# Expert stage of a transformer layer: TensorE in program order with whole blocks, last w2 loads ahead of the norm's, gain rows spread by a matmul

## The chip, the cores and the metric

The kernel runs on one core of one Trainium2 chip. A core has a matrix engine (TensorE, PE in the profile, with its weight loads shown as PEld), three engines for elementwise work (VectorE = DVE, ScalarE = ACT, GpSimd = POOL) and SyncE (SP), which here issues nearly all DMA transfers. The metric is device time in microseconds (us) of one execution of the whole layer.

## The reference

One trunk layer, fp32, 512 latent rows of 1024 channels and 256 context rows. First a token mixer (latent attention and differential attention side by side, gated, one output projection), then a norm, then a mixture of 16 experts with expert choice: each expert takes the 64 rows with its largest affinity.

```python
def ec_moe(h, w_router, b_router, w1, w3, w2):
    cap = EC_CAPACITY * n // N_EXPERTS                       # 64
    aff = softmax(h @ w_router + b_router)
    g, idx = lax.top_k(jnp.swapaxes(aff, 1, 2), cap)
    xe = h[bidx, idx]                                        # 16 experts x 64 rows x 1024
    hid = silu(xe @ w1) * (xe @ w3)                          # 1024 x 1024 each
    ye = (hid @ w2) * g[..., None]
    return zeros_like(h).at[bidx, idx].add(ye)

x = layer_norm(ALPHA * x + g1 * o_lat, ln1_g, ln1_b)         # g1, g2: gains by channel, from c
x = layer_norm(ALPHA * x + g2 * ec_moe(x * (1 + sc2) + sh2, ...), ln2_g, ln2_b)
```

The weights of the experts are 16 x 3 matrices of 4 MB, 201 MB in all; each is read once.

## The kernel before, in words

The first 574 us are the mixer, the output projection, the first norm and the router. From 574 us to the end runs the expert stage, which the change rewrites.

**Pairs.** Experts are worked through in eight pairs, since 2 x 64 rows fill the 128 rows of the array. For a pair:

- `gather`: a one-hot matrix `oh` (from DVE, L1094) multiplied with the normed rows `xn` puts the pair's rows, transposed, into `xe`: 32 products of 128x128 (L1102), 64 records in the trace.
- `up_`, once for each expert: 32 products (64 records) over sixteen pages of w1 and w3, with 64 columns of weights on half the array and 512 wide (L1140, `h<-wr,xe`); then Silu on ACT (L1145) and a product on DVE (L1146) make `hid`.
- `hid_t`: four transposes of `hid` on TensorE (L1151) and a copy by ACT (L1152) into `hidT`.
- `down`: `y<-wr,hidT` (L1159), again half the array, 16 products (32 records) an expert over eight pages.
- `back` and `scatter`: the one-hots times the gates are transposed (L1120, `ohT`); `y` is scaled by gate and by the gain row `g2b` on DVE (L1166), split into two float32r parts `ye` (ACT L75, DVE L78), and multiplied by `ohT` (L1171, whole array, 128x512): for each half of the columns four token tiles of two products. DVE adds each result tile into the accumulators `acc` (L1172).

The result tiles of gather, transposes and scatter are three PSUM buffers under one name, `mx`; `h` has three buffers too and `y` two.

**Weights.** They stream as pages of 512 KB through one DMA queue (SP's), in the order in which the products use them. 36 pages form a ring (buffers under four names); nine more lie at first in the places of tiles that are needed later (`acc0`, `ye`, `hid`, ...). `piece()` returns a page and, with `prefetch`, issues the load of the page that takes the place of one already used, so loads are issued as the program is written down and each waits on SP for its place to come free. The last pair's w2 comes by column parts (`PARTS`): 16 loads of 384 KB and 4 of 512 KB, so that each part of the output is complete as early as possible.

**The end.** Behind the last up product the tiles of `ln2_g` and `ln2_b` are loaded (L1222) into the places of `xe` and `hid`; then the last down product runs part by part (L1265), each part put back through the scatter (L1248), and the second norm follows.

**What sets the order.** The kernel is written in a tile framework. A scheduler orders each engine's instructions from their dependences and its own cost estimates; the program's order is only a preference. A DMA or an engine's instruction then runs strictly in its engine's order. The scheduler interleaves products of different steps on TensorE: records of the next pair's gather between those of the running pair's up product, and scatter products between those of the next up product.

**Rows by broadcast.** The gains `g1` and `g2` exist as single rows on partitions 0, 32, 64 and 96 of two tiles `rm`. GpSimd's library call `partition_broadcast` (L968 for `g1b`, L1187 for `g2b`) spreads them over 128 partitions. `g1b` is used in the output projection: its tiles `po` are sums over products of `yh`, `yl` with the split `w_out` pages `woh`, `wol`. For the first half of the columns DVE multiplies `po` by the gain (`r<-po,g1b`, L1007); for the second POOL scales the four `w_out` pages by it first (L888), and ACT and DVE split them (L75, L78). `xn` (L1008) is then normed, and transposed for the router (L1011). A half takes 96 products `po`.

Of the kernel before, what the change touches and what calls it, by code (L numbers as in the profile page):

```python
# [10 lines left out]
F32 = mybir.dt.float32  # L11
F32R = mybir.dt.float32r
# [40 lines left out]
def _layer(tc, A, out, opened):  # L53
# [32 lines left out]
    # ---------------------------------------------------------------- constants and small vectors  # L86
# [12 lines left out]
    ghv = cp.tile([128, KD], F32, name="ghv")       # routed input = ghv * normed + bhv  # L99
# [32 lines left out]
    dqs = [rB.tile([128, NT, 256], F32, name="dq", tag="dq", bufs=2) for _ in range(2)]      # two heads each  # L132
# [92 lines left out]
    def mod_mul(q):  # L225
        """scale and shift of 256 channels, as rows"""
# [21 lines left out]
    def x_chunk(k, ci):  # L248
        """128 channels of the latent (0) or context (1) rows: transposed, modulated, split"""
# [16 lines left out]
    for q in range(4):  # L266
        # beside the products of these channels: what makes the next
# [15 lines left out]
    # rotary tables: cos, signed sin for the keys; the query ones carry the score scale  # L283
# [42 lines left out]
    one32 = mw.tile([128, 32], F32, name="one32")  # L326
    V.memset(one32, 1.0)
# [20 lines left out]
    def mod_sum(j, wa):  # L348
# [3 lines left out]
        for g in (2 * h, 2 * h + 1):  # L352
            T.matmul(pm[32 * g:32 * g + 32, :], one32, wa[:, (g % 2) * 512:(g % 2) * 512 + 512], start=True, stop=True)
# [3 lines left out]
    def chunk(col, n, cuts, evac, at, nxt):  # L357
        """projected columns; after the tiles in `at`, a part of the modulation's rows"""
# [27 lines left out]
    # latent query and key ranks: rms norm, transpose, gain  # L386
# [55 lines left out]
    def gates(g4, at=()):  # L442
        """a quarter of the gates, transposed: weights stationary"""
# [52 lines left out]
    # score tiles are emitted one by one; between them goes the product work of the tiles before  # L496
# [13 lines left out]
    def fill(parts):  # L510
        """one score tile is out: emit one of `parts` equal shares of the waiting work"""
# [12 lines left out]
    def flush(key=None):  # L524
        """emit all the waiting work, or what has `key`"""
# [7 lines left out]
    # transposed queries and keys: even heads of the differential attention, then the latent ones | odd heads  # L533
# [21 lines left out]
    def prep_t(hd, m, nm, src, c0, t0, nn):  # L555
# [8 lines left out]
        if nm == "q1":  # L564
            # the same with the halves of the contraction swapped
# [13 lines left out]
    def mod_end():  # L579
# [13 lines left out]
        # router columns with the norm's gain, less their mean: the norm's own mean then drops out  # L593
# [744 lines left out]
```

## Time and profile before

Three executions took 1096.82, 1097.37 and 1098.73 us, median 1097.37. The profiled execution shows a span of 1094.2 us from its first to its last instruction; the page gives no other time of it.

| stretch, us | what runs | PE busy, us | DVE busy | GB/s |
|---|---|---|---|---|
| 0–440 | projections, attention | 415.61 | 242.60 | 122 |
| 440–574 | merge, output projection, norm, router | 108.14 | 76.95 | 216 |
| 574–1013 | expert pairs one to seven, start of the eighth | 429.94 | 105.47 | 396 |
| 1013–1045 | the eighth pair's up products | 30.24 | 3.79 | 15 |
| 1045–1094 | its down products, second norm | 23.44 | 26.00 | 206 |

Over the span TensorE is busy 92%, DVE 42%, ACT 25%, POOL 19%. How to read the rows further down: a timeline or waits row gives start, busy time, engine, line, operation, output<-inputs and shape, then xN for N instructions taken together, and in brackets the idle time ahead of the group and what ended it. A matrix product of fp32 operands appears as two records, one of float32r operands as one.

### The profile page before, as it was taken

Reading aid. Unit: us, or ns where it says so; the run is one execution under the profiler, and the core shown is the slowest. Engines: PE = TensorE matmul, PEld = TensorE weight load, DVE = VectorE, ACT = ScalarE, POOL = GpSimd, SP = SyncE. Lnnn points to the kernel's source line nnn. Section 1 sums busy time; section 2 is a strip of 40 time slices with the busy share of each in tenths; the row PEclk is TensorE's granted clock in tenths of the full one; section 3 lists DMA queues with packets and bytes.
Section 4 is the critical chain, followed back from the end, with each engine's and each line's share of the span. In section 5 each row is a group of like instructions: output and inputs, shape, how many; then the busy total and the mean of one; then the engine's idle time right before and its main releaser. Section 6 shows DMA issues by size and latency. Waiting matters only on the chain.

```text
span 1094.2 us, 13748 instructions
## 1 busy us (share of the span) xinstructions
PE 1007.4 (92%) x5259; PEld 630.1 (58%) x5259; DVE 454.8 (42%) x832; ACT 276.0 (25%) x551; POOL 204.4 (19%) x193
## 2 busy tenths in 40 slices
PE   6999998998899999997849999999999999999972
PEld 5888977677787777675536634444434434343331
DVE  2372377643677466463584221303022131303127
ACT  1222325244677455431210101010101010100001
POOL 2340022021675222143214200000000000000004
PEclk9999999999899999999889999999999999999997
DMA  9943357741002000176678999999999999999082
GB/s 302 288 154 106 97 169 247 243 140 39 20 20 74 20 20 21 39 269 235 245 270 304 404 329 411 409 409 409 409 409 409 409 410 408 409 410 400 14 283 97
DMA packets 101209, 266.97 MB, mean 244 GB/s; under 512 B 14020, under 2 KB 37528, under 8 KB 101144
## 3 DMA queue, kind: packets, MB, share of 16 engines
q1 hardware_dynamic: 100248, 264.52, 65.8%
q0 software_dynamic: 320, 1.05, 0.3%
q8 instruction: 41, 0.67, 0.3%
q10 hardware_dynamic: 576, 0.52, 0.1%
q14 instruction: 24, 0.20, 0.1%
HBM read 261.47 MB, written 2.10 MB: 241 GB/s over the span
## 4 chain that ended last, share of the span: by engine, by line
PE 75%; DVE 9%; DMA 5%; ACT 4%; issue 3%; POOL 2%; SPq 0%; DVEq 0%; ACTq 0%; POOLq 0%
PE h L1140 22%; PE y L1159 9%; PE mx L1102 6%; PE acc L84 4%; PE acc L83 4%; PE sc L648 4%; PE acc L82 4%; PE mx L1171 3%; PE tpb L656 3%; PE av L836 2%; DMA wa<-w_ada 2%; DMA wraw<-w_in 2%; PE y L1265 1%; PE av L772 1%; PE tp L232 1%
## 5 line engine op out<-in xcount | busy, mean ns | idle before, releaser
L1140 PE MATMUL h<-wr,xe 128*64 128x512 f32 x1024 | 250.0, 601 | 0.0
L1140 PEld LDWEIGHTS h<-wr,xe 128*64 128x64 f32 x1024 | 76.0, 136 | 110.4 <-issue 94.5
L1159 PE MATMUL y<-wr,hidT 128*64 128x512 f32 x448 | 99.6, 595 | 0.7 <-ACT hidT L1152 0.7
L1146 DVE TENSOR_TENSOR hid<-hid,h 128x512 f32<-128x512 f32 x16 | 11.0, 687 | 203.6 <-PE h L1140 203.6
L1102 PEld LDWEIGHTS mx<-oh,xn 128*128 128x128 f32 x512 | 62.7, 195 | 39.9 <-issue 38.7
L637 DVE TENSOR_REDUCE nm<-sc 128x1 f32<-128x768 f32 x64 | 61.0, 954 | 38.7 <-PE sc L648 38.2
L1115 POOL TENSOR_TENSOR oh<-oh,aff 128x512 f32<-128x512 f32 x8 | 8.4, 1049 | 361.9 <-PE mx L1102 353.1
L1102 PE MATMUL mx<-oh,xn 128*128 128x128 f32 x512 | 72.6, 289 | 1.7 <-DVE oh L1094 1.7
L1159 PEld LDWEIGHTS y<-wr,hidT 128*64 128x64 f32 x448 | 34.0, 137 | 57.8 <-issue 53.2
L638 ACT ACTIVATE P<-sc,nm 128x768 f32<-128x768 f32 x64 | 57.6, 900 | 35.0 <-DVE nm L637 26.0
L1145 ACT ACTIVATE hid<-h 128x512 f32<-128x512 f32 x16 | 9.6, 597 | 195.1 <-PE h L1140 195.1
L75 ACT ACTIVATE whi<-wraw 128x1024 fp32r<-128x1024 f32 (+1 forms) x32 | 33.5, 1046 | 99.6 <-DMA wraw<-w_in 80.9
L78 DVE TENSOR_TENSOR wlo<-wraw,whi 128x1024 fp32r<-128x1024 f32 (+1 forms) x32 | 38.7, 1211 | 43.9 <-PE acc L83 28.7
L82 PE MATMUL acc<-xlh,whi 128*128 128x512 f32 x128 | 51.0, 398 | 3.6 <-ACT whi L75 2.2
L82 PE MATMUL acc<-whi,xlh 128*128 128x512 f32 (+1 forms) x128 | 49.5, 391 | 1.0 <-ACT whi L75 1.0
L83 PE MATMUL acc<-xll,whi 128*128 128x512 f32 x128 | 50.0, 391 | 0.0
L84 PE MATMUL acc<-xlh,wlo 128*128 128x512 f32 x128 | 49.4, 394 | 0.3 <-DVE wlo L78 0.3
L84 PE MATMUL acc<-whi,xll 128*128 128x512 f32 (+1 forms) x128 | 48.8, 382 | 0.5 <-POOL xll L78 0.5
L83 PE MATMUL acc<-wlo,xlh 128*128 128x512 f32 (+1 forms) x128 | 48.8, 381 | 0.2 <-DVE wlo L78 0.2
L1172 DVE TENSOR_TENSOR acc<-acc,mx 128x512 f32<-128x512 f32 x56 | 36.0, 684 | 30.0 <-PE mx L1171 30.0
L648 PE MATMUL sc<-K,Q 96*128 96x512 f32 (+1 forms) x192 | 43.9, 355 | 1.3 <-ACT P L638 1.0
L820 POOL TENSOR_SCALAR P<-P,zm 128x768 f32<-128x768 f32 x32 | 30.0, 940 | 80.0 <-DVE zm L819 75.1
(333 smaller groups left out, 1691.4 us busy)
## 6 DMA issues: line engine op xcount, KB each, us to landing
wr<-moe_w SPq DMA_DIRECT2D x372, 512.0 KB, 10.2
wa<-w_ada SPq DMA_DIRECT2D x32, 512.0 KB, 4.0
wraw<-w_in SPq DMA_DIRECT2D x28, 512.0 KB, 4.7
wa<-w_ada SPq DMA_DIRECT2D x8, 1024.0 KB, 9.7
wr<-moe_w SPq DMA_DIRECT2D x16, 384.0 KB, 8.1
outraw<-w_out SPq DMA_DIRECT2D x8, 512.0 KB, 9.6
xq<-x SPq DMA_DIRECT2D x4, 512.0 KB, 7.9
q<-q SPq DMA_DIRECT2D x16, 128.0 KB, 2.3
```

The source lines that it names most:

```text
L75: S.activation(hi, src, AF.Copy)
L78: (eng_lo or V).tensor_tensor(lo, src, f(hi), op=OP.subtract)
L82: T.matmul(ps, lh, rh, start=start, stop=False)
L83: T.matmul(ps, lh, rl, start=False, stop=False)
L84: T.matmul(ps, ll, rh, start=False, stop=stop)
L637: V.tensor_reduce(nm, ps[:, :768], axis=AX.X, op=OP.max, negate=True)
L638: S.activation(p, ps[:, :768], AF.Exp, bias=nm, accum_out=z)
L648: T.matmul(ps[:, a:b], l, r[:, a:b], start=i == 0, stop=i == len(passes) - 1)
L1102: T.matmul(ps[:, kk * 128:(kk + 1) * 128], xn[t][:, k * 128:(k + 1) * 128], o[:, t].rearrange("p e s -> p (e s)"), start=t == 0, stop=t == ...
L1140: T.matmul(ph[i][64 * hf:64 * hf + 64, :], xe[:, k, sl], w[:, hf * 512:(hf + 1) * 512], start=k == 0, stop=k == KD - 1)
L1159: T.matmul(py[hf][r0:r0 + 64, :], hT[:, e % 2, fc % 4, fc // 4, :], w[:, hf * 512:(hf + 1) * 512], start=fc == 0, stop=fc == KD - 1)
L1172: V.tensor_tensor(acc[t][:, hs], acc[t][:, hs], ps, op=OP.add)
```

## The change

1. For the expert stage the scheduler is switched off for TensorE alone (`tc.manual_schedule`): it runs its instructions in the order in which the program writes them. The stage is rewritten so that this order is one of whole blocks. `gather` and `scatter` return lists of steps; `up_` takes a function that is called in the middle of its sixteen pages. In each pair from the second on: half of the first up product, the previous pair's scatter of column half 0, the second half of that up product, the scatter of column half 1, `back`'s transposes, the second expert's up product, `hid_t(0)`, the whole gather of the next pair, `hid_t(1)`, and both down products one behind the other.
2. `prefetch(len(order_r))` issues all remaining weight loads ahead of the second norm's two loads.
3. `spread()`, a matmul of one row of ones (a column of `one2`, a tile of ones, broadcast to 128) with the gain's row, and a copy by ACT, replace the four `partition_broadcast` calls. The modulation step's constant weights `one32` are replaced by the same broadcast column. Comments are removed.

```diff
+    def spread(dst, i, p, ps):
+        T.matmul(ps, one2[p:p + 1, 0:1].to_broadcast([1, 128]), rm[i][p:p + 1, :], start=True, stop=True)
+        S.activation(dst, ps, AF.Copy)
...
-            T.matmul(pm[32 * g:32 * g + 32, :], one32, wa[:, ...], start=True, stop=True)
+            T.matmul(pm[32 * g:32 * g + 32, :], one2[:, 0:1].to_broadcast([128, 32]), wa[:, ...], start=True, stop=True)
...
     for g in range(2):
-        G.partition_broadcast(g1b[:, g * 512:(g + 1) * 512], rm[0][32 * g:32 * g + 1])
+        spread(g1b[:, g * 512:(g + 1) * 512], 0, 32 * g, psc.tile([128, 512], F32, name="om", bufs=4))
...
-    def gather(pr, between=None):
+    def gather(pr):
...
+        def eighth(k):
+            hf, kk = divmod(k, 4)
+            if kk == 0:
+                pss[hf] = psd.tile([128, 512], F32, name="mx", bufs=3)
+            for t in range(NT):
+                T.matmul(pss[hf][:, kk * 128:(kk + 1) * 128], xn[t][:, k * 128:(k + 1) * 128], ...)
+            if kk == 3:
+                (four V.tensor_scalar into xe)
+        return xe, o, [lambda k=k: eighth(k) for k in range(KD)]
...
-    def up_(e, xe, hid, half=None):
+    def up_(e, xe, hid, between=None):
...
+        for k in range(KD):
+            if k == KD // 2 and between:
+                between()
...
-    def scatter(py, ohT, gt, g2b):
-        for hf in range(2):
+    def scatter(py, ohT, gt, hf):
...
+        def tile_(t):
+            ps = psd.tile([128, 512], F32, name="mx", bufs=3)
+            for i in range(2):
+                T.matmul(ps, ohT[:, hf, t * 128:(t + 1) * 128], ye[:, i, :], start=i == 0, stop=i == 1)
+            V.tensor_tensor(acc[t][:, hs], acc[t][:, hs], ps, op=OP.add)
+        return [lambda t=t: tile_(t) for t in range(NT)]
...
+    order_ = ExitStack()
+    order_.enter_context(tc.manual_schedule(engines={mybir.EngineType.PE}))
+    xe, o, steps = gather(0)
+    run(steps[:4])
+    waiting = None
+    for pr in range(E_N // 2):
+        last = pr == E_N // 2 - 1
+        hid = me.tile([128, 2, 512], F32, name="hid")
+        if waiting:
+            s0 = scatter(*waiting, 0)
+            up_(2 * pr, xe, hid, lambda: run(s0))
+            run(scatter(*waiting, 1))
+            ohT, gt = back(pr, o)
+        else:
+            up_(2 * pr, xe, hid, lambda: run(steps[4:]))
         up_(2 * pr + 1, xe, hid)
-        ohT, gt = back(pr, o)
+        if not waiting:
+            ohT, gt = back(pr, o)
         hT = me.tile([128, 2, 4, 2, CAP], F32, name="hidT")
-        py = [psd.tile([128, 512], F32, name="y", bufs=2) for _ in range(2)]
         hid_t(hid, hT, 0)
-        down(2 * pr, hT, py)
-        g_next = gather(pr + 1)
+        if last:
+            hid_t(hid, hT, 1)
+            break
+        xe, o, steps = gather(pr + 1)
+        run(steps)
+        hid_t(hid, hT, 1)
         if pr == 0:
             g2b = base()
-        hid_t(hid, hT, 1)
-        down(2 * pr + 1, hT, py)
-        scatter(py, ohT, gt, g2b)
...
+        py = [psd.tile([128, 512], F32, name="y", bufs=2) for _ in range(2)]
+        for i in range(2):
+            down(2 * pr + i, hT, py)
+        waiting = py, ohT, gt
+    prefetch(len(order_r))
     ln2 = []
...
     rest()
+    order_.close()
```

The order of TensorE's instructions round one scatter of a late pair, before: `h` is the next pair's up product, `mx<-ye,ohT` the scatter.

```order
L1159 MATMUL y<-wr,hidT 64x512 x30
L1171 MATMUL mx<-ye,ohT 128x512 x3
L1140 MATMUL h<-wr,xe 64x512
L1171 MATMUL mx<-ye,ohT 128x512 x3
L1140 MATMUL h<-wr,xe 64x512 x2
L1171 MATMUL mx<-ye,ohT 128x512 x2
L1140 MATMUL h<-wr,xe 64x512 x2
L1171 MATMUL mx<-ye,ohT 128x512 x3
L1140 MATMUL h<-wr,xe 64x512 x2
L1171 MATMUL mx<-ye,ohT 128x512 x3
L1140 MATMUL h<-wr,xe 64x512 x2
L1171 MATMUL mx<-ye,ohT 128x512 x2
```

The same place after the change, with the transposes of the one-hots (`mx<-ident,oh`) and of `hid`:

```order
L1160 MATMUL y<-wr,hidT 64x512 x32
L1144 MATMUL h<-wr,xe 64x512 x16
L1173 MATMUL mx<-ye,ohT 128x512 x8
L1144 MATMUL h<-wr,xe 64x512 x16
L1173 MATMUL mx<-ye,ohT 128x512 x8
L1124 MATMUL mx<-ident,oh 128x128 x4
L1144 MATMUL h<-wr,xe 64x512 x32
L1152 MATMUL mx<-ident,hid 128x128 x4
```

The sixteen scatter products stood in six pieces directly behind the down product; now they stand in two blocks, the first behind eight pages of the next up product, the second behind all sixteen.

SP's queue at the end of the program, before: the weight loads `wr` and the norm's two.

```order
L936 DMA wr<-moe_w 128x1024 x362
L934 DMA wr<-moe_w 128x2x384 x3
L1222 DMA ln_7468<-ln_g 128x1024
L1222 DMA ln_7470<-ln_b 128x1024
L934 DMA wr<-moe_w 128x2x384 x13
L934 DMA wr<-moe_w 128x4x256 x4
L1293 DMA out<-acc 128x768 x3
```

And after:

```order
L939 DMA wr<-moe_w 128x1024 x362
L937 DMA wr<-moe_w 128x2x384 x16
L937 DMA wr<-moe_w 128x4x256 x4
L1235 DMA ln_7516<-ln_g 128x1024
L1235 DMA ln_7518<-ln_b 128x1024
L1307 DMA out<-acc 128x768 x3
```

The norm's two loads moved behind 17 weight loads.

DVE ahead of the first norm, before: `wol` is the low part of a scaled `w_out` page, `r` the gated output tile, `xn` the residual rows.

```order
L78 TENSOR_TENSOR wol<-outraw,woh 128x1024 x2
L906 SCALAR_TENSOR_TENSOR yl<-ys,yh 128x512
L902 SCALAR_TENSOR_TENSOR gy<-th,om 128x512 x2
L906 SCALAR_TENSOR_TENSOR yl<-ys,yh 128x512 x2
L1007 TENSOR_TENSOR r<-po,g1b 128x512
L1008 SCALAR_TENSOR_TENSOR xn_4484<-xn_4484,r 128x512
```

And after:

```order
L905 SCALAR_TENSOR_TENSOR gy<-th,om 128x512 x2
L909 SCALAR_TENSOR_TENSOR yl<-ys,yh 128x512 x2
L78 TENSOR_TENSOR wol<-outraw,woh 128x1024 x2
L1010 TENSOR_TENSOR r<-po,g1b 128x512
L78 TENSOR_TENSOR wol<-outraw,woh 128x1024
L1011 SCALAR_TENSOR_TENSOR xn_4482<-xn_4482,r 128x512
```

Two splits of `w_out` pages moved to directly ahead of the first `r`, and one to between it and `xn`.

## Rows read from the trace of the kernel before

**Rows 1.** Busy us by stretch: window, length, engines, PEclk, DMA share, GB/s.
```profile
700.00:1000.00 300.00, 294.07 (x1392) 119.33 (x1394) 62.87 (x120) 29.43 (x59) 5.24 (x5) 1.00 1.03 409
1050.00:1055.00 5.00, 4.31 (x14) 2.12 (x16) 0.00 (x0) 0.00 (x0) 0.00 (x0) 0.68 1.01 366
```

**Rows 2.** Chain of waits, pairs' last down products: start us, us, what.
```profile
629.00 6.88 PE y L1159 x32
...
687.89 6.78 PE y L1159 x31
...
802.65 13.08 PE y L1159 x60
...
989.73 13.08 PE y L1159 x60
```

**Rows 3.** DMA issues, 700 to 1000 us: count, KB each, us to landing.
```profile
wr<-moe_w SPq DMA_DIRECT2D x234, 512.0 KB, 10.2
```

**Rows 4.** Timeline of TensorE, 900 to 920 us.
```profile
904.46 1.08 PE L1140 MATMUL h<-wr,xe 128*64 128x512 f32 x4
905.47 0.94 PE L1102 MATMUL mx<-oh,xn 128*128 128x128 f32 x6
906.34 1.08 PE L1140 MATMUL h<-wr,xe 128*64 128x512 f32 x4
```

**Rows 5.** Timeline of TensorE, 610 to 637 us.
```profile
620.82 6.74 PE L1102 MATMUL mx<-oh,xn 128*128 128x128 f32 x58
...
628.68 7.18 PE L1159 MATMUL y<-wr,hidT 128*64 128x512 f32 x32
```

**Rows 6.** Timeline of SP, 1000 to 1094 us.
```profile
1003.00 2.92 SPq L934 DMA_DIRECT2D wr<-moe_w  x3
1042.88 0.34 SPq L1222 DMA_DIRECT2D ln<-ln_g  x1
...
1045.06 16.62 SPq L934 DMA_DIRECT2D wr<-moe_w  x17
```

**Rows 7.** Timeline of TensorE, 1040 to 1076 us.
```profile
1045.15 1.51 PE L1265 MATMUL y<-wr,hidT 128*64 128x384 f32 x8
1050.69 6.42 PE L1265 MATMUL y<-wr,hidT 128*64 128x384 f32 x24 [4.03 <-DMA wr<-moe_w]
...
1062.46 4.08 PE L1265 MATMUL y<-wr,hidT 128*64 128x384 f32 x24
...
1070.86 0.96 PE L1248 MATMUL mx<-ye,ohT 128*128 128x384 f32 x4
1071.75 1.95 PE L1265 MATMUL y<-wr,hidT 128*64 128x256 f32 x16
```

**Rows 8.** Timeline of all engines, 1002 to 1009 us.
```profile
1002.79 1.42 DVE L1166 SCALAR_TENSOR_TENSOR y<-y,gate,g2b 128x512 f32<-128x512 f32 x2 [11.22 <-PE y L1159]
1003.59 0.60 ACT L75 ACTIVATE ye<-y 128x512 fp32r<-128x512 f32 x1 [13.22 <-DVE y L1166]
1004.22 0.69 DVE L78 TENSOR_TENSOR ye<-y,ye 128x512 fp32r<-128x512 f32 x1
1004.24 0.96 PE L1171 MATMUL mx<-ye,ohT 128*128 128x512 f32 x3 [1.48 <-ACT ye L75]
...
1006.67 1.88 DVE L1172 TENSOR_TENSOR acc<-acc,mx 128x512 f32<-128x512 f32 x3 [1.76 <-PE mx L1171]
```

**Rows 9.** DMA issues, 440 to 636 us.
```profile
wr<-moe_w SPq DMA_DIRECT2D x84, 512.0 KB, 5.7
```

**Rows 10.** Timeline of POOL, 496 to 530 us.
```profile
500.24 1.48 POOL L968 PARTITION_BROADCAST g1b<-rm  x2 [5.69 <-issue]
512.51 11.28 POOL L888 TENSOR_TENSOR outraw<-outraw,g1b 128x1024 f32<-128x1024 f32 x4 [10.79 <-issue]
```

**Rows 11.** Timeline of all engines, 520 to 526 us.
```profile
521.51 2.83 DVE L1008 SCALAR_TENSOR_TENSOR xn<-xn,r 128x512 f32<-128x512 f32 x1
...
524.39 1.11 PE L1011 MATMUL om<-ident,xn 128*128 128x128 f32 x4 [9.06 <-DVE xn L1008]
```

More of the change, by code (lines that the diff above doesn't have):

```diff
@@ L352, in mod_sum @@
         for g in (2 * h, 2 * h + 1):
-            T.matmul(pm[32 * g:32 * g + 32, :], one32, wa[:, (g % 2) * 512:(g % 2) * 512 + 512], start=True, stop=True)
+            T.matmul(pm[32 * g:32 * g + 32, :], one2[:, 0:1].to_broadcast([128, 32]), wa[:, (g % 2) * 512:(g % 2) * 512 + 512], start=True, stop=True)
             dma(bm[32 * g:32 * g + 32, :512], b_ada[4 + 4 * i + g:5 + 4 * i + g].to_broadcast([32, 512]))
@@ L1096, in gather @@
         xe = me.tile([128, KD, 128], F32, name="xe")
-        for hf in range(2):
-            ps = psd.tile([128, 512], F32, name="mx", bufs=3)
-            for kk in range(4):
-                k = 4 * hf + kk
-                for t in range(NT):
-                    T.matmul(ps[:, kk * 128:(kk + 1) * 128], xn[t][:, k * 128:(k + 1) * 128],
-                             o[:, t].rearrange("p e s -> p (e s)"), start=t == 0, stop=t == NT - 1)
-            for kk in range(4):
-                k = 4 * hf + kk
-                V.tensor_scalar(xe[:, k, :], ps[:, kk * 128:(kk + 1) * 128], ghv[:, k:k + 1], bhv[:, k:k + 1],
-                                op0=OP.mult, op1=OP.add)
-            if between:
-                between(xe, hf)
-        return xe, o
+        pss = {}
+        def eighth(k):
[3 more added lines that the diff above has]
+            for t in range(NT):
+                T.matmul(pss[hf][:, kk * 128:(kk + 1) * 128], xn[t][:, k * 128:(k + 1) * 128],
+                         o[:, t].rearrange("p e s -> p (e s)"), start=t == 0, stop=t == NT - 1)
+            if kk == 3:
+                for i in range(4):
+                    j = 4 * hf + i
+                    V.tensor_scalar(xe[:, j, :], pss[hf][:, i * 128:(i + 1) * 128], ghv[:, j:j + 1], bhv[:, j:j + 1],
+                                    op0=OP.mult, op1=OP.add)
+        return xe, o, [lambda k=k: eighth(k) for k in range(KD)]
     def back(pr, o):
@@ L1128, in back @@
         return ohT, gt
-    def up_(e, xe, hid, half=None):
+    def up_(e, xe, hid, between=None):
         sl = slice((e % 2) * CAP, (e % 2) * CAP + CAP)
-        if half == 1:
-            ph = first[0]
-        else:
-            ph = [psd.tile([128, 512], F32, name="h", bufs=3) for _ in range(2)]
-        for k in range(KD) if half is None else range(4 * half, 4 * half + 4):
+        ph = [psd.tile([128, 512], F32, name="h", bufs=3) for _ in range(2)]
+        for k in range(KD):
+            if k == KD // 2 and between:
+                between()
             for i, n in enumerate(("w1", "w3")):
@@ L1141, in up_ @@
                              start=k == 0, stop=k == KD - 1)
-        if half == 0:
-            first.append(ph)
-            return
         S.activation(hid[:, e % 2, :], ph[0], AF.Silu)
@@ L1160, in down @@
                          start=fc == 0, stop=fc == KD - 1)
-    def scatter(py, ohT, gt, g2b):
-        for hf in range(2):
-            hs = slice(hf * 512, (hf + 1) * 512)
-            ye = me.tile([128, 2, 512], F32R, name="ye")
-            V.scalar_tensor_tensor(py[hf], py[hf], gt[:, hf:hf + 1], g2b[:, hs], op0=OP.mult, op1=OP.mult)
-            split(ye[:, 0, :], ye[:, 1, :], py[hf])
-            for t in range(NT):
-                ps = psd.tile([128, 512], F32, name="mx", bufs=3)
-                for i in range(2):
-                    T.matmul(ps, ohT[:, hf, t * 128:(t + 1) * 128], ye[:, i, :], start=i == 0, stop=i == 1)
-                V.tensor_tensor(acc[t][:, hs], acc[t][:, hs], ps, op=OP.add)
+    def scatter(py, ohT, gt, hf):
+        hs = slice(hf * 512, (hf + 1) * 512)
+        ye = me.tile([128, 2, 512], F32R, name="ye")
+        V.scalar_tensor_tensor(py[hf], py[hf], gt[:, hf:hf + 1], g2b[:, hs], op0=OP.mult, op1=OP.mult)
+        split(ye[:, 0, :], ye[:, 1, :], py[hf])
+        def tile_(t):
[4 more added lines that the diff above has]
+        return [lambda t=t: tile_(t) for t in range(NT)]
     def base():
@@ L1186, in base, with run @@
         for g in range(2):
-            G.partition_broadcast(g2b[:, g * 512:(g + 1) * 512], rm[1][64 + 32 * g:65 + 32 * g])
+            spread(g2b[:, g * 512:(g + 1) * 512], 1, 64 + 32 * g, psd.tile([128, 512], F32, name="mx", bufs=3))
         return g2b
-    first = []
-    hid = me.tile([128, 2, 512], F32, name="hid")
-    g_next = gather(0, lambda xe, hf: up_(0, xe, hid, hf))
-    for pr in range(E_N // 2 - 1):
-        xe, o = g_next
-        if pr:
-            hid = me.tile([128, 2, 512], F32, name="hid")
-            up_(2 * pr, xe, hid)
+    def run(steps):
+        for fn in steps:
+            fn()
+    order_ = ExitStack()
[13 more added lines that the diff above has]
+            up_(2 * pr, xe, hid, lambda: run(steps[4:]))
         up_(2 * pr + 1, xe, hid)
-        ohT, gt = back(pr, o)
+        if not waiting:
+            ohT, gt = back(pr, o)
         hT = me.tile([128, 2, 4, 2, CAP], F32, name="hidT")
-        py = [psd.tile([128, 512], F32, name="y", bufs=2) for _ in range(2)]
         hid_t(hid, hT, 0)
-        down(2 * pr, hT, py)
-        g_next = gather(pr + 1)
+        if last:
[4 more added lines that the diff above has]
+        hid_t(hid, hT, 1)
         if pr == 0:
             g2b = base()
-        hid_t(hid, hT, 1)
-        down(2 * pr + 1, hT, py)
-        scatter(py, ohT, gt, g2b)
-    xe, o = g_next
-    ohT, gt = back(E_N // 2 - 1, o)
-    hid = me.tile([128, 2, 512], F32, name="hid")
-    hT = me.tile([128, 2, 4, 2, CAP], F32, name="hidT")
-    for i in range(2):
-        up_(E_N - 2 + i, xe, hid)
-        hid_t(hid, hT, i)
+        py = [psd.tile([128, 512], F32, name="y", bufs=2) for _ in range(2)]
[3 more added lines that the diff above has]
+    prefetch(len(order_r))
     ln2 = []
```

2 lines of the change are left out of this document (removed).

## The prediction

> **What bounds the kernel now.** I read the busy time by stretches first, then the chain of waits, then the expert stage engine by engine. From 700 to 1000 us two things are full at once: TensorE is busy 294.07 of 300 us, and the transfers move 409 GB/s at a DMA share of 1.03 [rows 1]. The chain gives the end of each pair's second down product: 629.00 + 6.88 = 635.9 for the first pair of experts, 694.7 for the second (58.8 later), 815.7 for the fourth, 1002.8 for the seventh [rows 2]. So pairs two to seven take 366.9 us, and the last three 62.4 each. The transfers alone want less: 234 pages of 512 KB are issued in 300 us, 1.282 us each [rows 3], so a pair's 48 pages take 61.5. TensorE sets the pace, narrowly, in the late pairs.
>
> Inside a late pair TensorE alternates: four records of an up product (half the array), then six of the gather (the whole array) [rows 4]. One turn is 906.34 − 904.46 = 1.88 us. An fp32 product leaves two records. In unmixed runs a half-array record takes (7.18 − 0.59)/31 = 0.213 us (0.59 is my reading of one record's own length) and a gather record 6.74/58 = 0.116 [rows 5]. The turn's work is 4 × 0.213 + 6 × 0.116 = 1.55, so its two changes of array shape cost 0.33 us, 0.17 each.
>
> At the end, the norm's two loads stand on SP's queue ahead of 17 of the last 20 w2 loads. Their tiles lie in places that the last up product still reads: nothing is issued from 1005.9 to 1042.88, the w2 loads follow at 1045.06 [rows 6], and TensorE, out of work at 1046.7, starts again at 1050.69 [rows 7].
>
> **The change part by part.** *Blocks on TensorE.* By the order of instructions a late pair before has about 39 changes of shape (12 round the scatter, some 22 round the gather, the rest at transposes), an early one 16; after, each has 6. Late: 33 fewer, 33 × 0.17 = 5.6. The idle 1.48 us ahead of the first scatter [rows 8] goes too, because eight weight pages of the next up product stand there now. Early: 10 fewer, 1.7.
> Blocks add a wait: eight scatter products write four PSUM tiles in turn, of three buffers, and DVE must add a tile away before the fourth can start. DVE adds three tiles in 1.88 us, 0.63 each; TensorE fills one in about 0.5 [rows 8]. In the first block DVE is free, and the fourth tile waits 0.2 at most. In the second, right behind an up product, ACT's Silu (0.6 like its other 512-wide pass) and DVE's product for `hid` (0.69, the form of the split's second half) [rows 8] come ahead of the adds: the first add ends about 2.5 us after the up product, the third tile is filled at 1.5, so the fourth waits about 0.9. Behind it stand the one-hots' transposes and the second expert's up product, which wait with it. I charge 1.0 a pair. No row shows such a block: it can cost 0 (if the adds keep pace) and at most 2 × 4 × 0.63 + 1.3 = 6.3, every add and the `hid` chain in full; I stay by 1.0, since products of 6.9 us stand ahead of each first add.
> From the late pair: 62.4 − 5.6 − 1.5 + 1.0 = 56.3. From the early pair: 58.8 − 1.7 + 1.0 = 58.1. I take 57.0 for each of pairs two to seven: 342, which is −24.9. The first pair's sequence hardly changes (two halves of down move behind the gather), and I leave 635.9.
>
> *Last up product.* Before: from 1002.8 to the first long run of the last down product at 1045.15 [rows 7], 42.3 us. After: 128 records × 0.213 = 27.3, two scatter blocks of about 2.2 with their changes, 1.0 wait, 0.6 for transposes, 0.5 for the rest, then 3.2 for Silu, the product, both hidden transposes and the four accumulator fills: 37.0 in all, −5.3.
>
> *The w2 loads ahead of the norm's.* With the loads there, the last down products run unwaited: 64 records × 0.17 (24 in 4.08) and 32 × 0.12 (16 in 1.95) are 14.8; two scatters of eight records (2 × 0.96 and a change of shape) [rows 7] 4.2; their chain through DVE and ACT 1.0: 20.0, instead of 1073.7 − 1045.15 = 28.55, so −8.5. Do the pages come in time? By 636, 84 are issued, at 5.7 us to landing [rows 9], so about 79 have landed. Page 368, the last of an up product, lands at 636 + 289 × 1.282 = 1006.5; the up product ends near 1011, with 4 pages to spare. The last 20 take 16 × 0.96 + 4 × 1.28 = 20.5 (by bytes): last landing 1027, and the last down record ends near 1035. It is close: with a pair at 55.6 or less TensorE would wait for transfers, which sets a floor: 1027 + 4 for the last pages' products + 20.5 of tail = 1051.5. The norm's rows are now issued behind the last w2 load, near 1018, and land by 1030 (two of 1.28 each behind some eight under way), ahead of the last down record. The tail from that record to the end, 1094.2 − 1073.7 = 20.5, stays.
>
> *Rows spread by matmul.* The POOL broadcasts go. Before, POOL sits idle 5.69 us ahead of them and 10.79 behind, then scales the w_out pages from 512.5 to 523.8 [rows 10]; TensorE waits 9.06 us in this stretch for an `xn` that DVE writes behind the page splits [rows 11]. After, scaling can start near 496.5, but by DVE's order two splits now stand ahead of the first `r`, and the transposes that need its `xn` stand after 39 instead of 45 of the 96 output products. POOL takes 11.28/4 = 2.8 a page here; so splits end near 502 and 505.5, `r` near 507, the third split 508.5, `xn` near 510. TensorE has done its 39 products by 500 and would wait 10 us there, 14 us earlier than it waited before, with six products (1.4) more left to do. The two nearly cancel in what the stage's end sees: POOL and DVE are late for the pages behind as before. I reckon 0 to −3. Bounds: −11 (both waits gone) and +4 (DVE later than I reckon). I take 0, since the trace's own wait is nearly the new one.
> In these rows DVE's `xn` at 521.51 takes 2.83 us [rows 11] while POOL scales a page. The Trainium skill (SBUF — State Buffer, "SBUF: two separate sides") says that DVE and GpSimd hold a shared port pair as an exclusive lock, the loser blocked for the whole instruction. The trace agrees, with that 2.83. By that rule the splits and the scaling keep taking turns when they move earlier, and the term is 0; without it DVE would be some 5 us sooner and the sum 5 lower.
> The second spread (g2, first pair) and the broadcast of a constant column as weights cost two or three products, each under 1 us like the widest one of [rows 8], beside waits that exist anyway.
>
> *Sum.* −24.9 − 5.3 − 8.5 + 0 = −38.7 on the span of 1094.2: 1055.5. The page gives no time of the profiled execution beyond its span; the median of the runs shown, 1097.37, is 3.2 over it, and I carry that over: 1059.
>
> **The rivals.** *Blocks wait as long as they save.* For: three PSUM buffers, and the adds are DVE's alone. Against: DVE is busy 62.87 of 300 us [rows 1]. Pairs stay at the early 58.8: 6 × 1.8 = 10.8 more, and about 1.5 in the last: 1071.
> *Transfers end last.* For: four pages to spare at the end of seven pairs. If three pages more are lost in the first 60 us, or a pair takes 55, TensorE waits page by page. After its 4 us wait at 1046.7 the granted clock was 0.68 for 5 us [rows 1], so the lower of its two levels, 1.2 GHz, was given for part of them; that adds 2 to 3. Floor 1051.5, plus 5 for the pages, 3 for the clock and 3.2: 1063. The Trainium skill (HBM Reference, "Specifications") gives about 358 GB/s as a core's share; as an estimate by that figure, 512 KB take 1.46 us, the pages left at 636 would end some 55 us later than I have them, and the kernel at about 1110. The trace's 409 speaks against it.
> *The front gives more.* Both waits of [rows 10, 11] shrink, and the lower clock behind them: −9, 1050.
> *Slower.* One mechanism: in the fixed order the second scatter block of a pair, and the up product queued behind it, wait for the whole chain through DVE and ACT: 0.7 for the gate product, 0.6 and 0.69 for the split, 1.3 for `hid`, 2.5 for four adds [rows 8], some 7 with hand-overs. It decides from 5.5 us a pair over the 1.0 that I charge (7 × 5.5 is the 38.7 gained); at 7 in full it is 7 × 6.0 = 42 beyond mine: 1101. Against: the split of either half is queued on DVE and ACT before the product ahead of the block ends.
> *The change doesn't do what it says*: the w2 loads wait for pages that only the last down product frees. Then −8.5 goes: 1067. Against: by the code 36 pages can be ahead of TensorE, and 20 are wanted.
>
> **How the numbers follow.** Forecast 0.6 (its own range 1050 to 1067), blocks that wait 0.14, transfers last 0.11, the front 0.07, loads held 0.03, slower 0.04, and 0.01 for no change. The range reaches from the floor less a few us of the front (1046) to the rival of 1071 and some, 1076, and leaves out the slower case, most of the no-change case and the tails of the others. Faster by over 0.2% (what measurements of this kernel can tell) is 0.95, same 0.01, slower 0.04.
>
> **What would show it.** Pair ends 57 us apart; waits of about 1 us ahead of the fourth scatter tile of each second block; SP's w2 loads without a gap, and near 409 GB/s until about 1027; no DMA wait over 2 us in the last down products; TensorE waiting between 500 and 510 for `xn`. I am wrong if pairs stay at 58 or more, if waits for pages appear from the fifth pair on, or if the front moves by more than 4 us.

## The result, and the profile after

The changed kernel takes 1065.5 us in the median (1062.8 to 1068.9) beside 1097.1 of the kernel before on the same chip: a ratio of 0.9716, 95% interval 0.9697 to 0.9734. The forecast was 1059, its own range 1050 to 1067; the rival "transfers end last" had said 1063. The time lies above both, 6.5 us over the first and 2.5 over the second, and the profile says that the mechanism is the rival's.

By stage, in the profiled executions (read from the starts and ends of the product groups; the last column is an experiment further down, whose transfers are fewer):

| stage, us | before | forecast | after | 16 pages fewer |
|---|---|---|---|---|
| start to the first gather product | 574.2 | 574.2 | 574.4 | 576.4 |
| first pair, to the end of its second down product | 61.7 | 61.7 | 64.8 | 64.7 |
| pairs two to seven | 366.9 | 342.0 | 338.8 | 328.6 |
| last up products, to the first long run of the last down | 42.3 | 37.0 | 42.5 | 36.1 |
| last down products | 28.6 | 20.0 | 22.2 | 20.9 |
| tail | 20.5 | 20.5 | 21.0 | 20.9 |
| span | 1094.2 | 1055.5 | 1063.7 | 1047.6 |

The stages of the changed kernel begin and end at these products (TensorE's timeline: start us, us, what):

```profile
574.37 6.66 PE L1107 MATMUL mx<-oh,xn 128*128 128x128 f32 x32 [1.19 <-DVE oh L1097]
...
625.26 13.96 PE L1160 MATMUL y<-wr,hidT 128*64 128x512 f32 x64
...
964.03 13.96 PE L1160 MATMUL y<-wr,hidT 128*64 128x512 f32 x64
...
1040.75 1.95 PE L1278 MATMUL y<-wr,hidT 128*64 128x256 f32 x16
```

The span's front moves by some us from one execution to the next, in stages that the change does not touch (the first gather product stands at 573 to 580 us in the profiled executions). Where single executions are compared below, I take the time from that product to the end: 520.0 us before, 489.3 after.

The chain of waits of the changed kernel through the third pair (start us, us, what) is a whole pair in a row:

```profile
693.98 6.87 PE h L1144 x32
700.85 2.18 PE mx L1173 x8
703.03 7.02 PE h L1144 x32
710.04 2.19 PE mx L1173 x8
712.24 0.58 PE mx L1124 x4
712.82 13.88 PE h L1144 x64
726.70 0.59 PE mx L1152 x4
727.29 7.15 PE mx L1107 x64
734.44 0.44 PE mx L1152 x4
734.88 13.88 PE y L1160 x64
748.76 1.28 PE h L1144 x5
```

Nothing but TensorE stands in it, and nothing waits: 748.76 − 693.98 = 54.8 us a pair, against 58.8 and 62.4 in [rows 2]. The gather is one run of 64 records in 7.15 us, where [rows 4] had it in pieces of six, and each scatter block is done in 2.2. From 639 to 858 us four pairs in a row keep 54.8. The next two take 57.6 and 62.1. What limits those can be seen on TensorE's timeline (start us, busy, group, then the idle time and what ended it), at the end of the last up products:

```profile
1011.11 1.08 PE L1144 MATMUL h<-wr,xe 128*64 128x512 f32 x4 [0.20 <-DMA wr<-moe_w]
1012.39 1.08 PE L1144 MATMUL h<-wr,xe 128*64 128x512 f32 x4 [0.20 <-DMA wr<-moe_w]
...
1016.25 1.08 PE L1144 MATMUL h<-wr,xe 128*64 128x512 f32 x4 [0.22 <-DMA wr<-moe_w]
...
1020.50 6.73 PE L1278 MATMUL y<-wr,hidT 128*64 128x384 f32 x34
...
1036.60 1.94 PE L1278 MATMUL y<-wr,hidT 128*64 128x256 f32 x14 [0.68 <-DMA wr<-moe_w]
```

A page, which is four records, starts every 1.28 us, the pace of the transfers in [rows 3]; unwaited, four records take 0.87. The last up page starts at 1016.25. The waits view of TensorE, 640 to 1045 us (us in total, times, longest), shows much less of it:

```profile
PE h L1144 <- DMA wr<-moe_w: 7.1, 34, 0.3
...
PE y L1278 <- DMA wr<-moe_w: 0.9, 2, 0.7
```

34 pages were waited for. By the spacing each cost 1.28 − 0.87 = 0.41, 14 us together; the view has 0.20 each, since the group ahead is drawn to its modelled end of 1.08. Groups of eight records hide a second wait inside them: by the table, pairs six and seven and the last up products take 16.5 us more than in the run with fewer pages. Small waits in great number are read from the spacing of the starts, not from this sum. Ahead of the pairs' scatter blocks (L1173) no wait is left.

SP's timeline at the end, beside [rows 6]:

```profile
1000.88 5.45 SPq L939 DMA_DIRECT2D wr<-moe_w  x5
1007.28 24.66 SPq L937 DMA_DIRECT2D wr<-moe_w  x20
1032.04 1.69 SPq L1235 DMA_DIRECT2D ln<-ln_g  x1
```

The w2 loads run without a gap, and the norm's two follow. So the queue is never held up at the end; it is simply the last to finish. Busy time by stretches, as in [rows 1]:

```profile
636.00:700.00 64.00, 64.00 (x330) 27.76 (x328) 15.16 (x28) 6.62 (x13) 1.05 (x1) 1.00 1.03 410
700.00:960.00 260.00, 255.42 (x1293) 110.24 (x1290) 60.39 (x114) 28.94 (x58) 4.19 (x4) 1.00 1.03 409
...
1020.00:1040.00 20.00, 18.39 (x96) 8.75 (x95) 7.52 (x22) 0.98 (x2) 0.00 (x0) 1.00 1.02 351
```

TensorE is full until 886 us, where the first wait for a page stands, in the sixth pair, and then waits; the transfers are full from 636 us on, and in the last stretch, at the same DMA share, move only 351 GB/s.

### The profile page after: what moved, and what is told of

It is laid out like the page before. It is cut to its first block, busy times and chain, and to the rows that moved or that the text cites. A ratio compares the mean times of both kernels' runs of the same rounds, so it can differ in the third digit from the quotient of the medians.

```text
span 1063.7 us, 13792 instructions
## 1 busy us (share of the span) xinstructions
PE 982.6 (92%) x5267; PEld 618.1 (58%) x5267; DVE 453.0 (43%) x831; ACT 278.2 (26%) x555; POOL 201.2 (19%) x189
## 4 chain that ended last, share of the span: by engine, by line
PE 63%; DMA 22%; DVE 8%; ACT 3%; POOL 2%; issue 2%; SPq 1%; DVEq 0%; ACTq 0%; POOLq 0%
DMA wr<-moe_w 17%; PE h L1144 12%; PE y L1160 7%; PE acc L84 5%; PE acc L82 5%; PE acc L83 5%; PE mx L1107 5%; PE sc L651 4%; PE tpb L659 3%; PE av L839 2%; DMA wa<-w_ada 2%; PE mx L1173 2%; PE av L775 1%; DMA wraw<-w_in 1%; PE po L84 1%
## 5 line engine op out<-in xcount | busy, mean ns | idle before, releaser
L1144 PE MATMUL h<-wr,xe 128*64 128x512 f32 x1024 | 233.8, 598 | 9.2 <-DMA wr<-moe_w 7.1
L1144 PEld LDWEIGHTS h<-wr,xe 128*64 128x64 f32 x1024 | 68.7, 137 | 163.1 <-issue 107.5
L1160 PEld LDWEIGHTS y<-wr,hidT 128*64 128x64 f32 x448 | 31.5, 137 | 61.8 <-issue 58.6
L641 ACT ACTIVATE P<-sc,nm 128x768 f32<-128x768 f32 x64 | 57.6, 899 | 33.6 <-DVE nm L640 25.5
L1107 PE MATMUL mx<-oh,xn 128*128 128x128 f32 x512 | 61.8, 284 | 1.4 <-DVE oh L1097 1.4
L75 ACT ACTIVATE ye<-y 128x512 fp32r<-128x512 f32 (+2 forms) x17 | 9.7, 572 | 179.8 <-DVE y L1167 98.7
L1167 DVE SCALAR_TENSOR_TENSOR y<-y,gate,g2b 128x512 f32<-128x512 f32 x14 | 9.9, 754 | 92.6 <-PE y L1160 92.6
L1112 DVE TENSOR_SCALAR xe<-mx,ghv,bhv 128x128 f32<-128x128 f32 x64 | 21.9, 404 | 55.5 <-PE mx L1107 55.5
## 6 DMA issues: line engine op xcount, KB each, us to landing
wr<-moe_w SPq DMA_DIRECT2D x372, 512.0 KB, 10.2
```

What stands on the lines that cost most here:

```text
L641: S.activation(p, ps[:, :768], AF.Exp, bias=nm, accum_out=z)
L1107: T.matmul(pss[hf][:, kk * 128:(kk + 1) * 128], xn[t][:, k * 128:(k + 1) * 128], o[:, t].rearrange("p e s -> p (e s)"), start=t == 0, stop ...
L1144: T.matmul(ph[i][64 * hf:64 * hf + 64, :], xe[:, k, sl], w[:, hf * 512:(hf + 1) * 512], start=k == 0, stop=k == KD - 1)
L1160: T.matmul(py[hf][r0:r0 + 64, :], hT[:, e % 2, fc % 4, fc // 4, :], w[:, hf * 512:(hf + 1) * 512], start=fc == 0, stop=fc == KD - 1)
```

## The experiments

**Does the w2 order carry its term alone?** The kernel before with one line added:

```diff
+    prefetch(len(order_r))
     ln2 = []
```

> The kernel before with one line of the change: all weight loads are issued ahead of the second norm's two. Theory (transfers end last in the changed kernel, since only some 71 pages had landed at 636 us, not 79; here TensorE still sets the pace at 62.4 us a pair, so pages are in stock at the end): the wait of 4 us ahead of the last down product goes, and the term of -8.5 shows nearly in full, 1088 to 1090 us. Rival (the last down products are limited by something else than the late loads): 1094 or more.

Measured: ratio 0.9942 (0.9923 to 0.9962), some 6.4 us less, where 8.5 was the term; the median, 1092.0 us, is 2 us over the range of the theory and 2 under that of the rival. TensorE's timeline (first fence) and SP's (second):

```profile
1050.44 5.38 PE L1266 MATMUL y<-wr,hidT 128*64 128x384 f32 x32
1057.12 0.62 PE L1249 MATMUL mx<-ye,ohT 128*128 128x384 f32 x2 [1.29 <-ACT ye L75]
```

```profile
1008.64 23.73 SPq L934 DMA_DIRECT2D wr<-moe_w  x20
1048.17 0.34 SPq L1223 DMA_DIRECT2D ln<-ln_g  x1
```

No product waits for a page any more, and the stretch from 1050.44 to the last down record is 22.1 us. So the wait went as said; the 20.0 for an unwaited stretch was about 2 too short.

**And taken away again?** The changed kernel without that line.

> The changed kernel without that line: the norm's two loads stand ahead of 17 w2 loads again and wait for the last up product, near 1017 us. Theory (transfers end last): the queue then stands still from about 1008 to 1018, and all of that is added to the end: 1075 to 1077 us. Rival (TensorE's own order sets the end, the waits for pages only stand in for others): the loads cost what they cost before, 28.5 - 22.2 = 6 us: 1070 to 1072.

Measured: ratio 0.9755 (0.9727 to 0.9783), 1070.2 us, some 4 to 5 more than the changed kernel. That is near the rival's number. SP's timeline shows where the expected standstill went:

```profile
1011.51 2.93 SPq L937 DMA_DIRECT2D wr<-moe_w  x3
1021.54 0.34 SPq L1234 DMA_DIRECT2D ln<-ln_g  x1
...
1023.73 17.15 SPq L937 DMA_DIRECT2D wr<-moe_w  x17
```

The queue stands from 1014.4 to 1021.5, but some eight loads were still under way (10.2 us from issue to landing is eight of 1.28), so the transfers themselves never stopped: in windows of 2 us they moved 137 to 350 GB/s between 1018 and 1030, which is some 4 us of the full pace. My number for the theory had forgotten these. The run does not tell the two theories apart.

**Do transfers end last?** The changed kernel with 16 of the 384 pages not loaded; the products read another page instead, so that the output is not the layer's:

```diff
-    order_r = [i for i in range(len(order)) if i not in places]
+    order_r = [i for i in range(len(order)) if i not in places and not (order[i][1] == "w3" and order[i][2] == KD - 1)]
...
     def piece(e, nm, k):
+        if (nm, k) == ("w3", KD - 1):
+            return kept[0]
```

> The changed kernel without the loads of 16 of its 384 weight pages: the last page of each expert's w3 is not loaded, its products read the page of w1 instead (this changes what is computed), so TensorE has exactly the same work and 16 x 1.28 = 20.5 us of transfers are gone. Theory (transfers end last; TensorE alone would need 54.8 us for every pair, some 36 for the last up product and 20 to 22 for the last down products): waits for pages vanish up to the last pair, 1045 to 1051 us. Rival (TensorE's order sets the end): 1062 or more.

Measured: ratio 0.9525 (0.9507 to 0.9544), 1048.8 us. Every pair now takes 54.8 us, the sixth and seventh too; the chain has

```profile
901.06 13.88 PE y L1164 x64
...
955.84 13.88 PE y L1164 x64
```

and no wait of an up product for a page is left. With the same products TensorE alone needs 471 us from the first gather product, the changed kernel takes 489. That settles it: its last 18 us are transfers'.

**Why are so few pages in stock?** By the queue's own pace one can count back: the last up page was worked on at 1016.25, where the forecast had it landed at 1006.5. That is 9.75 us late, 7.6 pages: about 71 had landed at 636, not 79. The busy time by stretches of the changed kernel shows where transfers nearly stood still (last two columns: DMA share, GB/s):

```profile
615.00:620.00 5.00, 4.83 (x43) 4.59 (x42) 2.00 (x6) 2.83 (x7) 0.00 (x0) 1.00 1.03 413
620.00:625.00 5.00, 5.00 (x36) 3.87 (x34) 2.28 (x7) 0.99 (x2) 1.05 (x1) 1.00 0.42 168
625.00:630.00 5.00, 5.00 (x23) 1.64 (x24) 0.00 (x0) 0.80 (x2) 0.00 (x0) 1.00 0.53 161
```

This is the first pair's gather for the next, 7.4 us in which no page comes free, with the ring full, and behind it the spread of `g2b`, 1.9 more. In the waits of SP, one load stands 11.0 us until a down product frees its place. In the kernel before the first down product stood ahead of the gather ([rows 5] has the gather from 620.82), and the longest such wait is 7.5 us. So I moved it back, in the first pair only:

```diff
+        py = [psd.tile([128, 512], F32, name="y", bufs=2) for _ in range(2)]
+        if pr == 0:
+            down(0, hT, py)
         xe, o, steps = gather(pr + 1)
         run(steps)
...
-        for i in range(2):
+        for i in range(pr == 0, 2):
```

> The changed kernel with the first pair's first down product moved ahead of the next pair's gather, as it stood in the kernel before; all other pairs unchanged. Theory (transfers end last, and stand still between 614 and 625 us because all pages of the ring are full and no product frees one): down's eight pages come free some 10 us sooner, the queue goes on, and of the 6 to 8 us of standstill most is gained at the end: 1057 to 1061 us, at 82 or more loads issued by 62 us after the first gather. Rival (the standstill is made up for later, or TensorE sets the end): 1064 to 1067, a change of shape or two the worse.

Measured: ratio 0.9668 (0.9654 to 0.9683), 486.2 us from the first gather product against 489.3. The gain is there but is 3 to 5 us; the median, 1064.1 us, lies at the edge of the rival's range, since the kernel before took 1100.3 beside it. Not more loads were issued by that mark (79): the standstill had half moved to behind the gather.

```profile
625.00:630.00 5.00, 5.00 (x47) 5.00 (x47) 1.37 (x4) 0.00 (x0) 0.00 (x0) 1.00 1.03 410
630.00:635.00 5.00, 5.00 (x30) 3.04 (x30) 1.37 (x4) 1.79 (x3) 1.05 (x1) 1.00 0.67 265
635.00:640.00 5.00, 5.00 (x26) 1.72 (x24) 0.00 (x0) 0.00 (x0) 0.00 (x0) 1.00 0.73 237
```

So next the gather went behind both down products of the first pair (`down(0)`, `hid_t(1)`, `down(1)`, `base()`, then the gather), beside the changed kernel as it is:

> The changed kernel as it is, once more, on the same chip as the next two, so that they can be compared with it: 0.968 to 0.973 of the time before.

> The changed kernel with the first pair's gather for the second pair behind both of its down products (the run with one of them ahead still shows transfers at 265 and 237 GB/s from 630 to 640 us, some 4 us of standstill). Theory (transfers end last and every page that is freed sooner counts until the queue is never out of places): 6 to 9 us less than the changed kernel in the same call, some 2 to 4 less than with one product ahead. Rival (the new waits, for the second hidden transpose and for the gathered rows ahead of the next up product, eat it, or TensorE sets the end): within 3 us of the changed kernel.

Measured: the changed kernel 0.9723 (0.9699 to 0.9747), the edited one 0.9663 (0.9639 to 0.9687), 1065.3 and 1060.0 us. From the first gather product 489.0 and 481.8 us; up to 1.5 of that difference can be the clock at its start, since the first 32 gather records took 6.76 us in the one execution and 5.19 in the other. The standstill is gone, 84 loads are issued by 62 us after that product instead of 80, although TensorE now waits there, 0.83 and 0.69 us for two hidden transposes:

```profile
630.00:635.00 5.00, 5.00 (x32) 2.58 (x29) 1.09 (x2) 1.34 (x3) 0.00 (x0) 1.00 1.02 409
635.00:640.00 5.00, 5.00 (x48) 5.00 (x47) 2.39 (x6) 0.34 (x1) 0.00 (x0) 1.00 1.03 408
```

This version beats both kernels: the changed one by 5 to 7 us. What the second down product adds to the first is not sure: 4.4 us from the first gather product, but the ratios, 0.9663 and 0.9668, do not differ by more than their intervals.

**Do short rows slow the last loads?** The last pair's w2 in two column parts:

```diff
-PARTS = (0, 384, 2), (384, 384, 2), (768, 256, 4)
+PARTS = (0, 512, 2), (512, 512, 2)
```

> The changed kernel with the last pair's w2 in two column parts of 512 (two chunks a page, rows of 2 KB in memory) in place of 384, 384 and 256 (rows of 1.5 and 1 KB). Theory (the last 20 loads ran at 351 GB/s and not 409 because their rows are short, which costs 2 to 3 us at an end that transfers set): the last landing comes 2 us sooner, and the second norm's last part, twice as wide, costs 2 to 4 us more: 1064 to 1068 us, with a stretch of the last loads at 380 GB/s or more. Rival (something else slows these loads, as the norm's two loads beside them): 351 GB/s as before, 1067 to 1070.

Measured: ratio 0.9691 (0.9677 to 0.9705), 490.1 us from the first gather product (after: 489.3). SP's timeline:

```profile
1005.90 20.51 SPq L937 DMA_DIRECT2D wr<-moe_w  x16
```

The same bytes are issued in 20.51 us instead of 24.66. Issues follow the landings of loads some eight places ahead, so both figures take in pages of 4 KB rows; where the new rows alone land, the pace is not the full one, but it is well over the 351 GB/s above:

```profile
1020.00:1035.00 15.00, 14.69 (x61) 5.17 (x61) 5.55 (x15) 0.60 (x1) 0.00 (x0) 1.00 1.04 385
```

By the packets in the traces, the last w2 load lands 462.6 us after the first gather product instead of 464.5. The last down record ends 465.1 us after the first gather product instead of 468.3. The tail behind it is 25.0 us instead of 21.0, since the last part of the norm is twice as wide. Both halves of the theory are seen: the rows do cost some 2 us at the last landing and 3 at the last product, and the cure costs 4 at the end. The median, 1066.4 us, is in its range.

**Is it the blocks?** The changed kernel without `manual_schedule`:

```diff
-    order_.enter_context(tc.manual_schedule(engines={mybir.EngineType.PE}))
```

> The changed kernel with one line taken out: the scheduler orders TensorE's instructions again, from the rewritten program. Its order mixes gather and scatter with the up products as before (a piece of gather between every two up products). Theory (the gain of 28 us over six pairs comes from whole blocks on TensorE, the rewriting alone gives none): late pairs take 62 us again, TensorE sets the pace, the loads ahead of the norm's remain a gain: 1088 to 1095 us. Rival (the program's new sequence of steps carries the gain): 1065 to 1075.

Measured: ratio 0.9875 (0.9858 to 0.9891), 1086.9 us, just under the range that I gave the theory. The second and third pair take 55.7 us, the last four 62.7. The chain in a late one:

```profile
967.94 1.01 PE h L1144 x4
968.95 0.87 PE mx L1107 x6
969.82 1.01 PE h L1144 x4
970.83 0.87 PE mx L1107 x6
```

The turn of 1.88 us of [rows 4] is back, and with it the wait of 1.5 us ahead of each scatter. The order alone is worth some 17 us of the 31 (0.9875 − 0.9716), although the kernel with it is held back by its transfers. Against the theory, the rewriting gives something without the order too: of the 13.7 us that this run gains the w2 line alone gives 6.4, and the second and third pair are 3 us shorter than the early 58.8.

**The spread.** The kernel before with the spreads alone, and the changed kernel with GpSimd's broadcasts back.

```diff
-        G.partition_broadcast(g1b[:, g * 512:(g + 1) * 512], rm[0][32 * g:32 * g + 1])
+        spread(g1b[:, g * 512:(g + 1) * 512], 0, 32 * g, psc.tile([128, 512], F32, name="om", bufs=4))
```

> The kernel before with the gain rows spread by a matmul instead of by GpSimd, nothing else. Theory (the stage's wait is as long as before, only earlier; the spread of the second gain costs TensorE about 2 us in the first pair): 1097 to 1099 us. Rival (the wait of 9 us on TensorE near 515 to 524 shrinks): 1088 to 1094.

> The changed kernel with GpSimd's broadcasts of both gain rows back in place of the two matmuls. Theory (the front is worth 0; transfers end last, so 1.9 us less on TensorE in the first pair count only by what pages come free sooner): 1063.5 to 1066.5 us, no difference beyond 0.2%. Rival (the spread is worth a gain of its own in the changed kernel): 1068 or more.

Measured: 1.0016 (0.9997 to 1.0035) for the spread alone, and 0.9698 (0.9675 to 0.9721) with the broadcasts back in the changed kernel, which has 0.9716 and 0.9723. Neither differs from its partner by more than the intervals. Single executions, from the first gather product, show a cost of the spread all the same: 524.3 us with it alone against 520.0 before (1.4 of this is a slower clock in the first gather, 38 records in 7.42 us against 6.00), and 486.9 with the broadcasts in the changed kernel against 489.3 and 489.0. So do SP's waits for a down product in the first pair, the longest of which is 7.5 us before, 11.4 with the spread alone, 11.0 in the changed kernel, and 8.7 there with the broadcasts. The same exchange in the fastest version:

> The run above with GpSimd's broadcasts in place of the two spreads by matmul. Theory (1.9 us of TensorE in the first pair go, transfers end last, so only the pages that come free sooner count): 0 to 2 us less than the run above. Rival (the spread is worth a gain): 1 to 3 us more.

Measured: 0.9665 (0.9645 to 0.9686), no different from 0.9663. The first pair is 1.9 us shorter on TensorE with the broadcasts (62.9 instead of 64.8 in the run with them in the changed kernel), but in the run times no part of that is sure at the end. In the fastest version, where the longest of those waits is 2.4 us, 482.7 and 481.8 us from the first gather product show none of it either.

## Why the prediction was right and where it failed

**Blocks.** Right in kind, too small in size: a pair of 57.0 was forecast, one of 54.8 measured wherever pages were there. The term that was mis-sized is the wait of 1.0 us charged for the second scatter block; there is none. The timeline of all engines:

```profile
709.23 0.60 ACT L1146 ACTIVATE hid<-h 128x512 f32<-128x512 f32 x1 [5.57 <-PE h L1144]
709.98 2.26 PE L1173 MATMUL mx<-ye,ohT 128*128 128x512 f32 x8
710.16 0.69 DVE L1147 TENSOR_TENSOR hid<-hid,h 128x512 f32<-128x512 f32 x1 [5.53 <-PE h L1144]
710.77 2.47 DVE L1174 TENSOR_TENSOR acc<-acc,mx 128x512 f32<-128x512 f32 x4
```

I had put Silu and the product for `hid` one behind the other after the up product, 1.3 us. But Silu needs w1's sum only, and starts at 709.23, before the last products of w3 are out; the first add is done some 1.4 us behind the up product and not 2.5 (710.77 and a quarter of 2.47, from 709.98), before the third tile is filled. The rest is that I settled between the estimate from a late pair (56.3) and that from an early one (58.1), though both end in the same sequence. For the mixing I had 0.17 us a change of shape: 62.4 − 54.8 − 1.5 of idle time over 33 changes is 0.185. The Trainium skill (TensorEngine Tiling (Array Packing), "Key Properties") says that a change of the tiling mode drains TensorE; the trace shows that price for a change between half and whole array, and not whether the engine drains there.

**First pair.** Failed, a little: it was left at 61.7 and takes 64.8. The spread for `g2b` stands in the fixed order (1.88 us for four records), and waits of 0.67, 0.50 and 0.38 us stand ahead of its up products, where the scheduler had filled in other work (TensorE was busy 61.63 of the first 62 us, now 59.91). The prediction had put the spread "beside waits that exist anyway"; it stands on the path of the down products, and with the broadcasts the pair takes 62.9. Some 1 us is neither: the granted clock of the first 6 us was 0.50 here and 0.72 in the execution before, so the first 32 gather records took 6.66 us, the next 32 3.84.

**Transfers, the step that failed.** "With 5.7 us to landing about 79 have landed" was wrong twice. The 5.7 is a median from 440 to 636 us [rows 9], most of which is a queue that is not full; a full one has eight loads under way, 10.2 us as in [rows 3], so that 84 issued means 76 landed. And the 84 are of the kernel before: the changed one had issued 80 by then, because its first pair frees pages later. I had read the new order and priced it on TensorE only ("hardly changes"), not on the queue, which the pair's pages feed. Two things delay them, the move of both down products behind a gather and the spread. Counted 90 us after the first gather product, when all queues are full, the loads issued are 105 before, 102 in the changed kernel, 104 with the broadcasts back in it, 102 with the spread alone, and 107 with both down products ahead of the gather; so the spread seems to have at least as large a part in the loss as the move; these are single executions, and a page more or less is not sure. Page 368 came 9.75 us later than I had it. The second miss is the last 20 loads, 20.5 us by bytes at the full pace; their short rows land at 351 GB/s, and it takes 22.6 us from 1016.25 to the last packet at 1038.8. Together they put the last landing 12 us behind my 1027, and the last up products, forecast at 37.0, stay at 42.5, with pairs six and seven 2.8 and 7.3 longer. Waits for pages from the fifth pair on were my own sign of being wrong; they came from the sixth.
The two errors pull against each other: TensorE was some 10 us faster than I had it, the transfers 12 slower. That the time came out inside the likeliest case's own range is in part luck. The rival "transfers end last" named the cause (pages lost in the first 60 us, a pair at 55) at 0.11; seen from here it deserved more than the forecast, since its own condition, a pair at 55.6 or less, was only 0.7 below the late pair's estimate. Its sum came near for partly other reasons: it allowed 3 us for a lower clock, but the granted clock stayed at 1.00 to 1040 us, and it lost three pages where about eight were missing. The HBM figure of 358 GB/s that I set beside it is, in the same section of the Trainium skill (HBM Reference, "Specifications"), the share with both cores of a pair streaming, and a core alone is given about 425; the trace shows 409 from 636 to 1010 us.

**w2 ahead.** Right: without a gap on SP, no wait for a page over 0.7 us in the last down products. Worth 6.4 alone and 4 to 5 in the changed kernel, not 8.5, since the 20.0 for an unwaited stretch was too short: alone it is 22.1, with two waits of 1.29 and 1.30 us for `ye` where I had 1.0 for the whole chain; in the changed kernel 22.2, with 0.9 us of page waits.

**Front.** Right in place and size. The wait went from 515–524 to 500–510:

```profile
506.36 0.68 DVE L1010 TENSOR_TENSOR r<-po,g1b 128x512 f32<-128x512 f32 x1
506.96 2.76 DVE L78 TENSOR_TENSOR wol<-outraw,woh 128x1024 fp32r<-128x1024 f32 x1
509.64 0.68 DVE L1011 SCALAR_TENSOR_TENSOR xn<-xn,r 128x512 f32<-128x512 f32 x1
...
510.58 1.09 PE L1014 MATMUL om<-ident,xn 128*128 128x128 f32 x4 [10.50 <-DMA wr<-moe_w]
```

`r` ends at 507.0 and `xn` at 510.3, where 507 and 510 were reckoned from DVE's order and POOL's 2.8 us a page; the wait is 10.5 (the view names a load, but the transposes read `xn`, which ends just ahead). The first gather product stands at 574.4 instead of 574.2; since it moves by up to 7 us between executions, the term of 0 rests on the run of the spread alone (1.0016) more than on this. The `xn` that took 2.83 us beside one of POOL's pages [rows 11] takes 0.68 here, where POOL is done at 508.6.

## What to carry to other kernels

When TensorE and the transfers are nearly level, a change that speeds one up is priced by both, from the stock of pages at a stated time: count loads landed, that is issued less those under way in a full queue, and follow the stock to the end. A block that frees no page, like the gather or the spread, put where the ring is full stops the queue, and a queue that is the bound at the end never makes this up; such blocks go behind the products that free pages. And a page-by-page limit shows as the spacing of the groups' starts (1.28 us), of which a sum of waits can show half.

## What the runs showed of the hardware

Rows shorter than 4 KB in memory cost the queue pace even when it is full, at a DMA share of 1.02 to 1.07: 409 GB/s for rows of 4 KB, 385 for 2 KB, 375 from 1014 to 1026 us in the changed kernel, where nearly all rows are of 1.5 KB, and 345 from 1031 to 1035, where most are of 1 KB. The loads of 1 KB rows hold 512 KB like a full page, so it is not the size of a load. The Trainium skill (Perfetto Trace Analysis, "DMA Optimizations") speaks of a significant overhead for DMAs below 2 KB; taken by the row, the runs agree, and show some 6% already at 2 KB.
